# A hybrid decoder layer on one core: the token mix's projections as 2x2 block products in seven multiplications

## The chip, the cores and the metric

The kernel runs on one core of a Trainium2 chip. The metric is the device time of one execution in microseconds (us). Five engines work side by side, each with its own instruction stream: PE (matrix products), DVE and POOL (elementwise work), ACT (copies and activations) and SP, which here only issues DMAs. A core has 16 DMA engines that all queues share.

## The reference, cut to what matters

One layer on 512 prompt tokens and 64 sample tokens (8 sequences of 8), 576 tokens in all, model width 1024, everything in fp32: a half-step SwiGLU feed-forward (FFN1), a token mix, a second feed-forward (FFN2). A conditioning vector gives nine modulation vectors per sequence (`m`, 9 x 1024 columns, 18 strips of 512).

```python
m = silu(c) @ w_ada + b_ada                      # sh1 sc1 g1 sh2 sc2 g2 sh3 sc3 g3
x = x + 0.5 * g1 * swiglu(modulate(rms_norm(x, n1_g), sh1, sc1), w1_gate, w1_up, w1_down)
h = modulate(rms_norm(x, nm_g), sh2, sc2)
z = h @ w_in                                     # 1024 x 10240
u, v, q, k, rv, rg, ga, gb = split(z)            # 1024 1024 1024 1024 2048 2048 1024 1024
o_a = gelu(u) * chunk_spatial_mix(layer_norm(gelu(v)), gm_ws, gm_bs)
o_r, S_new = retention(rotary(q), rotary(k), rv, S0)         # 8 heads, dk 128, dv 256
o_b = head_rms(o_r) * silu(rg)
x = x + g2 * ((sigmoid(ga) * (o_a @ w_a) + sigmoid(gb) * (o_b @ w_b)) @ w_o)
x = x + 0.5 * g3 * swiglu(modulate(rms_norm(x, n2_g), sh3, sc3), w2_gate, w2_up, w2_down)
```

Outputs are the normalised x, the new retention states and the sample rows of the normalised v.

## The kernel before, in words

**Arithmetic.** Activations lie transposed on chip, features on the 128 partitions and tokens along the row. Each fp32 operand is kept as a high and a low part in the PE's faster format (fp32r), and a product is three matmuls: high by high, high by low, low by high. ACT writes the high part (a cast), DVE subtracts to get the low part (L141 and L142 for plain weights, L697 and L707 in the feed-forwards, L149 and L150 for activations). The 576 tokens are taken in two halves of 288, so a block of 128 output columns is 2 x 8 x 3 = 48 matmuls of 128x288 (`proj`, L516, matmul line L522).

**The feed-forwards** already multiply 2x2 blocks. `Operands` builds, once per feed-forward, sums and differences of the four blocks of the activations (1024 features in two halves, 576 tokens in two halves). A `Pair` takes one gate and one up block of 128 columns, forms the sums s1 to s4 of its weight blocks on DVE, and needs seven products P1 to P7 of 12 matmuls (`prod`, L675, matmul line L679) where two `proj` blocks need eight: 84 matmuls for 96. The first two pairs are `Plain`, with eight products, because they come while the operands are still being built. The last product of a pair, p4, is issued only after the next pair's first products.

**The token mix** uses `proj` and two wider forms. Per head (`project`, L1193, eight times): q, k and two blocks of rg by `proj`, 4 x 48 matmuls; then rv with the tokens as the stationary side, 96 matmuls of 128x256 (L1236) and 16 more for the sample tokens (L1244, from the tile `hs`). While head h + 1 is projected, the generator `core` of head h (scores, state update, the norm over the head, the product with silu(rg)) hands out its pieces: each matmul group calls `tick(us)` with a nominal time, and a generator whose pause has run down issues its next piece there. Then `out_b` multiplies head h by its 256 rows of w_b, 16 groups of 6 matmuls, and DVE adds each group to the tile `acc` (L1421, a copy at L1419 for the first head). After the heads, v is made by 192 matmuls of 128x512 and 32 for the sample tokens (L1452), u and the gates ga and gb by `proj` again, and w_a and w_o follow.

**The modulation strips** (`ada_strip`, L295) are a generator too. A strip is four loads of 512 KB, eight groups of matmuls (L265), a copy M by ACT (L271) and four transposes on PE (L277). Two tiles in turn hold loads and copies, so a load waits on its queue until the products of the load two before it are done. Strips 0 to 3 come at the start, 4 and 5 with a pause of 3, strips 6 to 9 in FFN1 with a pause of 12, and 10 to 17 in the token mix with a pause of 20. A strip's generator pauses three and a half times, so at a pause of 12 one lasts about 40 nominal us. `finish(gen)` issues all that is left of a generator at once, with nothing between; `last_down1` (L1098), the last part of FFN1, begins with `finish(rest)`.

**Order.** A scheduler puts each engine's instructions in the order in which the program issues them, apart from three stretches written out by hand as step tables: `BEGIN`, `INTO_MIX` (FFN1's last product, the norm, the operands of the token mix) and `INTO_FFN2`. DMAs issued on SP stand in the program's order and wait there for their buffers. Of a raw weight tile (`wraw`) there are three buffers, of a split one (`whl`) four, and the token mix has one more `whl`.

## Time and profile before

| | |
|---|---|
| time, median of 3 executions | 1718.4 us (1717.9 to 1719.52) |
| the profiled execution | 1718.67 us, its span 1716.6 us |
| PE busy | 1683.7 us (98%), 12588 matmuls |
| DVE busy | 1049.4 us (61%) |
| ACT busy | 686.6 us (40%) |
| POOL busy | 209.0 us (12%) |
| DMA | 199.52 MB, 116 GB/s on average, 38.4% of 16 engines in the main queue |

The span is what the profile records; the execution is 2.1 us longer. FFN1's last products end near 456 us, the heads' projections run from there to about 964 us, then come v, u, the gates and, to about 1255 us, w_a; w_o and FFN2 follow. A matmul's duration overlaps its neighbours', so what a row of matmuls costs is read as the distance from its first start to the next row's start, divided by its count.

### The profile page before, as it was taken

What the parts mean: (1) busy time and instruction counts of PE and PEld (TensorE: products, weight loads), DVE (VectorE), ACT (ScalarE), POOL (GpSimd) and SP (SyncE); (2) the same over time, 40 slices, a digit from 0 to 9 for tenths busy, and PEclk for the clock granted to TensorE, in tenths of its full rate; (3) what the DMA queues carried; (4) which work ended last, traced back from release to release, by engine and by line L of the source; (5) the groups of instructions that cost most, each with busy time, mean ns of one, the idle gap of its engine ahead of it and who ended that gap; (6) DMA issues with size and microseconds to landing.
All of it is one profiled execution on the core that took longest, in us unless ns stands there. A gap on an engine that the chain in (4) does not pass through costs nothing.

```text
span 1716.6 us, 30444 instructions
## 1 busy us (share of the span) xinstructions
PE 1683.7 (98%) x12588; PEld 1610.9 (94%) x12588; DVE 1049.4 (61%) x1758; ACT 686.6 (40%) x1137; POOL 209.0 (12%) x263
## 2 busy tenths in 40 slices
PE   7999999999999999999999999999999999999997
PEld 4879999999999999999999889999999999999997
DVE  6856847676765745745745546422547958666773
ACT  5533524335534333333333333322235525344354
POOL 0000000000421302302202101220021000000002
PEclk9999999999999999999999999999999999999999
DMA  9443444323454433444424335342330323323231
GB/s 301 132 145 98 134 139 129 99 87 95 146 163 140 142 115 125 132 123 125 149 83 143 100 115 161 103 154 75 99 103 21 87 80 92 99 84 89 86 99 56
DMA packets 279773, 199.52 MB, mean 116 GB/s; under 512 B 9801, under 2 KB 253769, under 8 KB 279634
## 3 DMA queue, kind: packets, MB, share of 16 engines
q1 hardware_dynamic: 279634, 197.58, 38.4%
q8 instruction: 98, 1.61, 0.4%
q14 instruction: 41, 0.34, 0.1%
HBM read 183.12 MB, written 14.42 MB: 115 GB/s over the span
## 4 chain that ended last, share of the span: by engine, by line
PE 88%; DVE 4%; DMA 4%; ACT 2%; issue 1%; SPq 0%; POOL 0%; POOLq 0%; DVEq 0%; ACTq 0%
PE ps L522 47%; PE ps L679 24%; PE ps L1236 5%; PE ps L1452 3%; PE ps L265 2%; DMA wraw<-in_w_down_dram 1%; DMA ada<-in_w_ada_dram 1%; DVE whl L707 1%; PE ps L1366 1%; PE ps L1244 1%; PE ps L1328 1%; DMA xa<-in_w_ada_dram 1%; ACT whl L697 1%; PE ps L1372 1%; PE ps L1344 0%
## 5 line engine op out<-in xcount | busy, mean ns | idle before, releaser
L522 PE MATMUL ps<-xa,whl 128*128 128x288 f32 x2784 | 378.4, 295 | 0.5 <-DVE whl L142 0.3
L522 PEld LDWEIGHTS ps<-xa,whl 128*128 128x128 f32 x2784 | 370.9, 188 | 7.6 <-issue 3.4
L679 PE MATMUL ps<-xa,whl 128*128 128x288 f32 x2064 | 292.8, 296 | 1.9 <-ACT whl L697 1.0
L679 PEld LDWEIGHTS ps<-xa,whl 128*128 128x128 f32 x2064 | 279.1, 188 | 10.5 <-issue 2.5
L142 DVE TENSOR_TENSOR whl<-wraw,whl 128x1024 fp32r<-128x1024 f32 x100 | 126.2, 1270 | 212.4 <-ACT whl L141 208.4
L522 PE MATMUL ps<-c,wd 128*128 128x288 f32 x1824 | 246.7, 295 | 0.0
L522 PEld LDWEIGHTS ps<-c,wd 128*128 128x128 f32 x1824 | 243.2, 188 | 2.6 <-issue 1.7
L679 PE MATMUL ps<-xs,whl 128*128 128x288 f32 x1680 | 239.7, 296 | 1.6 <-ACT sn L688 1.4
L679 PEld LDWEIGHTS ps<-xs,whl 128*128 128x128 f32 x1680 | 228.5, 188 | 7.5 <-ACT sn L688 4.9
L522 PE MATMUL ps<-c,whl 128*128 128x288 f32 x1368 | 194.9, 298 | 0.0
L522 PEld LDWEIGHTS ps<-c,whl 128*128 128x128 f32 x1368 | 184.1, 188 | 2.7 <-DVE S L1391 0.8
L141 ACT CAST whl<-wraw 128x1024 fp32r<-128x1024 f32 x100 | 104.0, 1046 | 107.3 <-PE ps L522 47.6
L509 POOL TENSOR_TENSOR x<-x,s 128x64 f32<-128x64 f32 x72 | 34.4, 478 | 909.4 <-DVE s L508 909.2
L503 DVE SCALAR_TENSOR_TENSOR x<-ps,gate,x 128x288 f32<-128x288 f32 (+1 forms) x128 | 61.5, 483 | 135.3 <-PE ps L522 134.9
L697 ACT CAST whl<-sum 128x1024 fp32r<-128x1024 f32 x80 | 84.0, 1050 | 86.3 <-DVE sum L832 58.2
L707 DVE TENSOR_TENSOR whl<-sum,whl 128x1024 fp32r<-128x1024 f32 x80 | 98.0, 1225 | 30.2 <-ACT whl L697 28.2
L697 ACT CAST whl<-wraw 128x1024 fp32r<-128x1024 f32 (+1 forms) x84 | 70.6, 841 | 98.5 <-PE ps L679 84.8
L1236 PEld LDWEIGHTS ps<-whl,xa 128*128 128x128 f32 x768 | 94.1, 194 | 5.1 <-DVE whl L142 3.4
L1236 PE MATMUL ps<-whl,xa 128*128 128x256 f32 x768 | 95.6, 286 | 3.2 <-DVE whl L142 3.2
L909 ACT CAST wd<-wraw 128x640 fp32r<-128x640 f32 (+2 forms) x58 | 45.3, 782 | 123.6 <-PE ps L522 116.7
L707 DVE TENSOR_TENSOR whl<-wraw,whl 128x1024 fp32r<-128x1024 f32 (+1 forms) x84 | 81.2, 967 | 9.5 <-ACT whl L697 9.1
L688 ACT COPY sn<-ps 128x288 f32<-128x288 f32 x126 | 50.1, 398 | 59.2 <-PE ps L679 57.7
(264 smaller groups left out, 1835.2 us busy)
## 6 DMA issues: line engine op xcount, KB each, us to landing
wraw<-in_w_in_dram SPq DMA_DIRECT2D x80, 512.0 KB
ada<-in_w_ada_dram SPq DMA_DIRECT2D x56, 512.0 KB
wraw<-in_w_gate_dram SPq DMA_DIRECT2D x88, 256.0 KB
wraw<-in_w_up_dram SPq DMA_DIRECT2D x88, 256.0 KB
wraw<-in_w_down_dram SPq DMA_DIRECT2D x32, 384.0 KB
wraw<-in_w_down_dram SPq DMA_DIRECT2D x32, 320.0 KB
S<-in_state_ret_dram SPq DMA_DIRECT2D x32, 256.0 KB
wraw<-in_w_b_dram SPq DMA_DIRECT2D x16, 512.0 KB
```

Of the source, the lines that this page charges most:

```text
L141: ACT.copy(out=hi, in_=raw)
L142: (eng or DVE).tensor_tensor(out=lo, in0=raw, in1=hi.bitcast(F32), op=ALU.subtract)
L503: DVE.scalar_tensor_tensor(out=x[:, o:o + w], in0=ps[:, :w], scalar=g[:, c, 0:1], in1=x[:, o:o + w], op0=ALU.mult, op1=ALU.add)
L509: return lambda: POOL.tensor_tensor(out=x[:, NP:T], in0=x[:, NP:T], in1=u, op=ALU.add)
L522: PE.matmul(ps[:, :H], lhsT=s[:, k, c0:c0 + P], rhs=m[:, HALF[h]], start=k == 0 and z == 0, stop=k == kc - 1 and z == 2,)
L679: PE.matmul(ps[:, :H], lhsT=s[:, j * P:(j + 1) * P], rhs=m[:, j, :], start=fresh and j == 0 and z == 0, stop=j == 3 and z == 2, skip_group ...
L688: ACT.copy(out=t, in_=ps[:, :H])
L697: ACT.copy(out=hl[:, 0], in_=src)
L707: DVE.tensor_tensor(out=hl[:, 1], in0=src, in1=hl[:, 0].bitcast(F32), op=ALU.subtract)
L909: ACT.copy(out=hl[:, 0], in_=self.raw[c])
L1236: PE.matmul(ps[:, :DV], lhsT=s, rhs=m, start=i == 0, stop=i == 23)
L1452: PE.matmul(ps, lhsT=s, rhs=m[:, kx % 2, :], start=kx == 0 and z == 0, stop=kx == KC - 1 and z == len(terms) - 1,)
```

## The change

- **Projections.** `Pair2` and `Plain2` extend the feed-forward's classes: the same seven (or eight) products, with the results handed to `out` and `post` in place of gate times up. w_in's 80 column blocks become 40 pairs: q with k, the two rv blocks and the two rg blocks of each head, and neighbouring blocks of u, v, ga and gb. The first two (rg and rv of head 0) are `Plain2`, 38 are `Pair2`. `stream(p)` issues a pair and leaves its last product p4 to be issued by `behind()` inside the next pair, or in `out_b`, `mix` or the w_a products.
- **rv and v** now come out with features on the partitions, like q and k, and PE transposes turn them: 10 per head (`turn_rv`), 40 for v (`turn_v`). ACT copies the results out.
- **Rotary** reads three of a pair's four results from a tile in SBUF that DVE first wrote (`less`), the fourth from PSUM.
- **Operands on chip.** `Operands` for the token mix works in place in x1's tile. x1 is saved to memory before that by 16 DMAs on ACT's queue (steps `sp`), where before 8 DMAs on SP did it later. `Modulate`, `block` and `hs` go. `INTO_MIX` is written anew: it builds the operands and runs the first three pairs.
- **Sums over heads in memory.** `out_b` copies each result with ACT into a tile t (two buffers of 590 KB, 4 groups each) and sends it to the memory tile accd: plain on SP for head 0, with addition on the way on POOL's queue for heads 1 to 7, 28 such DMAs. The 128 DVE operations of L1419 and L1421 go. `gate_b` loads the sums back.
- **Modulation strips.** Strips 6 to 17 all belong to FFN1, with a pause of 8.
- **Weight sums.** S, U and V are written in place into the raw weight tiles, one more DVE operation of 128x512 and one fewer of 128x1024 in every pair, the feed-forwards' too; the tile `sum` goes. The token mix loses its extra `whl`; its raw tiles stay three.

```diff
-    rest = ada_rest(range(6, 10), 12.0)
+    rest = ada_rest(range(6, 18), 8.0)
     start(first_gate, 4.0)
     start(rest, 70.0)
...
         def S(self):
-            self.sum = now["raw"].tile([P, 2, 512], F32, tag="sum", name=nm("sum"), bufs=1)
-            DVE.tensor_tensor(
-                out=self.sum, in0=self.q[:, 1:2].broadcast_to([P, 2, 512]), in1=self.p, op=ALU.add
-            )
+            DVE.tensor_tensor(out=self.p[:, 1], in0=self.q[:, 1], in1=self.p[:, 1], op=ALU.add)
+            DVE.tensor_tensor(out=self.q[:, 1], in0=self.q[:, 1], in1=self.p[:, 0], op=ALU.add)
...
+    class Pair2(Pair):
+        def less(self, i, h, ps, t):
+            out = self.out(i, h)
+            DVE.tensor_tensor(out=out, in0=ps[:, :H], in1=t, op=ALU.subtract)
+            self.post(i, h, out)
...
+    def stream(p, begun=False):
+        if not begun:
+            p.splits()
+            p.p1()
+            p.p1s()
+            p.p2()
+        behind()
+        p.e2()
+        if not begun:
+            p.p5()
+            p.p5s()
+            p.p6()
+            p.p6s()
+        p.p3()
+        p.p7()
+        held.append(p.p4)
...
     def project(hd):
-        ws = w0 if hd == 0 else [load_w(win, 0, KC, head_cols(hd, i), P) for i in range(4)]
+        head = Head(hd) if hd else head0
+        stream(pairs[3] if hd == 0 else head.pair("qk"), hd == 0)
...
-            start(ada_rest(range(10, 18), 20.0), 20.0)
...
+            stream(head.pair("rv"))
+            stream(head.pair("rg"))
+        rv, rvs = turn_rv(head.rv)
...
     def out_b(hd, OB):
         for j in range(2):
             wb = load_w(a["w_b"][0], 2 * hd, 2, j * 512, 512)
             for c in range(4):
+                if c % 2 == 0:
+                    t = tks["tk"].tile([P, 2, T], F32, tag="t", name=nm("t"), bufs=2)
                 for h in range(2):
                     ps = proj(wb, OB, h, kc=2, c0=c * P)
-                    dst = acc[4 * j + c][:, HALF[h]]
+                    behind()
+                    ACT.copy(out=t[:, c % 2, HALF[h]], in_=ps[:, :H])
+                    tick(cost(2))
+                if c % 2:
+                    dst = accd[:, 4 * j + c - 1:4 * j + c + 1, :]
                     if hd == 0:
-                        DVE.tensor_copy(out=dst, in_=ps[:, :H])
+                        nc.sync.dma_start(out=dst, in_=t)
                     else:
-                        DVE.tensor_tensor(out=dst, in0=dst, in1=ps[:, :H], op=ALU.add)
-                    tick(cost(2))
+                        POOL.dma_start(out=dst, in_=t, accum_op=ALU.add)
```

The lines of the changed kernel have other numbers: the strips' products L263, its loads L299, its transposes L275, `prod` L616, `proj` L450, low parts of weights L644, the weight sums S, U and V L754 to L767, `less` L862, rotary L1126 to L1128, the norm over the head L423 to L425 and L1419.

How the strips stand on PE. Before, in FFN1's fourth group, the first half of the last strip (`ada` are its two loads) between the products of the last pairs:

```order
L679 MATMUL ps_3352<-xa_363,whl_3336 128x288 x12
L265 MATMUL ps_3194<-ada_3195,cs 32x512 x2
L265 MATMUL ps_3194<-ada_3196,cs 32x512 x2
L679 MATMUL ps_3375<-xs_78_463,whl_3339 128x288 x12
L679 MATMUL ps_3224<-xa_502,whl_3208 128x288 x12
```

After, on PE at the end of FFN1, the first three rows being the last products ahead of `finish(rest)` (8 of the 12 strips and half of the ninth stand ahead of these rows):

```order
L450 MATMUL ps_4623<-c_4587,wd_4571 128x288
L450 MATMUL ps_4623<-c_4588,wd_4571 128x288
L450 MATMUL ps_4623<-c_4587,wd_4571 128x288
L263 MATMUL ps_4639<-ada_4648,cs 32x512 x2
L263 MATMUL ps_4639<-ada_4649,cs 32x512 x2
L275 MATMUL ps_4658<-ident,ada_4656 128x128 x4
L263 MATMUL ps_4666<-ada_4667,cs 32x512 x2
L263 MATMUL ps_4666<-ada_4668,cs 32x512 x2
L263 MATMUL ps_4666<-ada_4675,cs 32x512 x2
L263 MATMUL ps_4666<-ada_4676,cs 32x512 x2
L275 MATMUL ps_4685<-ident,ada_4683 128x128 x4
L263 MATMUL ps_4693<-ada_4694,cs 32x512 x2
```

The second half of one strip and three whole strips now stand back to back; two more strips of the same form (L263 four times, L275) follow these rows before the next product of FFN1. And on SP, after, the loads for them:

```order
L133 DMA wraw_4761<-in_w_down_dram 128x6x128
L299 DMA ada_4667<-in_w_ada_dram 128x2x512
L299 DMA ada_4668<-in_w_ada_dram 128x2x512
L299 DMA ada_4675<-in_w_ada_dram 128x2x512
L299 DMA ada_4676<-in_w_ada_dram 128x2x512
L299 DMA ada_4694<-in_w_ada_dram 128x2x512
```

Twelve such loads stand together, with no other load among them; the first weights of the token mix come behind the twelfth.

How DVE stands between two heads. Before, where the norm of head 1 (product with silu(rg) L1407, its low parts L150) meets the rotary products of head 2 (L1186 to L1188):

```order
L1407 TENSOR_TENSOR h_6408<-h_6408,h_6397 128x288
L150 TENSOR_TENSOR c_6372<-h_6403,c_6371 128x288
L1186 TENSOR_TENSOR h_6438<-ps_6413,rope 128x288
L150 TENSOR_TENSOR c_6374<-h_6408,c_6373 128x288
L1187 TENSOR_TENSOR h_6439<-ps_6413,rope 64x288
L1188 TENSOR_TENSOR h_6439<-ps_6413,rope 64x288
L282 TENSOR_REDUCE m_6449<-ps_6444 128x36
```

After, the end of the same stretch between heads 5 and 6: it begins with L423 of head 5's norm, 37 rows ahead of the last row here, and holds the sums and low parts for head 6's rv pair (the last of them `whl_9716`) among the rotary of its q and k pair:

```order
L1126 TENSOR_TENSOR h_9695<-h_9692,rope 128x288
L1127 TENSOR_TENSOR h_9696<-h_9692,rope 64x288
L1128 TENSOR_TENSOR h_9696<-h_9692,rope 64x288
L754 TENSOR_TENSOR wraw_9701<-wraw_9702,wraw_9701 128x512
L862 TENSOR_TENSOR c_9769<-ps_9738,sn_9736 128x288
L755 TENSOR_TENSOR wraw_9702<-wraw_9702,wraw_9701 128x512
L1126 TENSOR_TENSOR h_9763<-ps_9594,rope 128x288
L758 TENSOR_TENSOR wraw_9701<-wraw_9701 128x512
L1127 TENSOR_TENSOR h_9764<-ps_9594,rope 64x288
L767 TENSOR_TENSOR wraw_9702<-wraw_9701,wraw_9702 128x512
L1128 TENSOR_TENSOR h_9764<-ps_9594,rope 64x288
L644 TENSOR_TENSOR whl_9716<-wraw_9701,whl_9716 128x1024
```

The four 128x512 sums of the next pair's weights and their low part stand behind the rotary operations; before, DVE had no weight sums in the token mix.

More of the change, by code (lines that the diff above doesn't have):

```diff
@@ L1110, in last_down1 @@
             steps[f"Wl{c}"] = lambda c=c: W.lo(c)
[L1111 to L1120 removed]
+        now["wraw"] = None
+        p = {0: head0.plain("rg", 0), 1: head0.plain("rv", 1), 2: head0.pair("qk")}
+        pairs[3] = p[2]
+        steps.update(operand_steps(O))
+        ends = pair_steps(p, None)
+        for n in ("Gh0", "Gl0", "Gh1", "Gl1", "e1s1", "e1m1"):
+            ends.pop(n)
+        steps.update(ends)
         for c, h in LAST:
@@ L1581, in layer_kernel @@
     second = layer_norm(1, 2.5)
-    for g in range(AHEAD):
-        gate_u(g)
-    gate_b(0)
-    for g in range(8):
-        if g == 1:
-            start(second, 0.0)
+    gate_u(0)
+    gate_u(2)
+    start(second, 0.0)
+    for g in range(0, 8, 2):
         if g == 4:
             finish(second)
+        if g < 4:
+            gate_u(g + 4)
+        else:
+            behind()
         mix(g)
-        if g + AHEAD < 8:
-            gate_u(g + AHEAD)
-        else:
-            gate_b(g + AHEAD - 7)
-    for c in range(4, KC):
-        gate_b(c)
+        mix(g + 1)
+    finish()
     st.close()
```

617 lines of the change are left out of this document (288 added, 329 removed).

## The prediction

> **What bounds the kernel now.** First the page: the span, busy times, slices, the chain.
>
> ```profile
> span 1716.6 us, 30444 instructions
> PE 1683.7 (98%) x12588; PEld 1610.9 (94%) x12588; DVE 1049.4 (61%) x1758; ACT 686.6 (40%) x1137; POOL 209.0 (12%) x263
> PE   7999999999999999999999999999999999999997
> PE 88%; DVE 4%; DMA 4%; ACT 2%; issue 1%; SPq 0%; POOL 0%; POOLq 0%; DVEq 0%; ACTq 0%
> ```
>
> PE is full from the second slice to the last and carries 88% of the chain. A matmul saved is a gain wherever nothing else waits in its place, and any wait put on PE's queue is a loss in full. The profiled execution took 1718.67 us, 2.1 more than its span and 0.3 from the median, so I sum on the span and add 2.1.
>
> Next, the timeline of PE gives the price of each shape: from a row's first start to the next row's start, over its count.
>
> ```profile
> 1204.01 51.04 PE L522 MATMUL ps<-c,whl 128*128 128x288 f32 x384
> 1254.89 12.88 PE L522 MATMUL ps<-xa,whl 128*128 128x288 f32 x96
> ...
> 603.67 11.66 PE L1236 MATMUL ps<-whl,xa 128*128 128x256 f32 x96
> 615.17 2.05 PE L1244 MATMUL ps<-whl,hs 128*128 128x256 f32 x16
> 617.06 1.22 PE L522 MATMUL ps<-c,whl 128*128 128x288 f32 x8
> ...
> 668.81 11.76 PE L1236 MATMUL ps<-whl,xa 128*128 128x256 f32 x96
> ...
> 970.51 11.08 PE L1452 MATMUL ps<-whl,xa 128*128 128x512 f32 x48
> 981.52 1.06 PE L265 MATMUL ps<-ada,cs 128*32 128x512 f32 x8
> ...
> 39.25 0.60 PE L277 MATMUL ps<-ident,ada 128*128 128x128 f32 x4
> 39.60 0.64 PE L679 MATMUL ps<-xa,whl 128*128 128x288 f32 x3
> ```
>
> So 288 wide: 50.88/384 = 0.1325 us. 256 wide: 11.50/96 = 0.120 and 1.89/16 = 0.118. 512 wide: 11.01/48 = 0.229. A transpose: 0.35/4 = 0.09. A head takes 668.81 − 603.67 = 65 us.
>
> **Term 1, the products.** Before, q, k, rg, u, ga and gb are 56 blocks of 48, 2688 matmuls of 288. After, 2 plain pairs of 96 and 38 of 84 make 3384, 696 more: +92.2 us. Gone are 8 x 96 of L1236 (92.0), 8 x 16 of L1244 (15.1) and v's 224 of 512 (51.4): −158.5. Added are 10 transposes a head and 40 for v, 120, at 0.09 to 0.12 (an estimate): +12. Term 1 is **−54 us**; per head, 252 x 0.1325 + 1.0 = 34.4 where 38.8 stood.
>
> **Term 2, the strips at the end of FFN1.** The order shows three and a half strips back to back on PE with nothing between, and twelve loads back to back on SP. Each load waits for one of two tiles, that is for PE or for the copy M. What a load costs when PE waits for it:
>
> ```profile
> 82.10 9.64 SPq L301 DMA_DIRECT2D ada<-in_w_ada_dram  x3
> ...
> 87.62 1.05 PE L265 MATMUL ps<-ada,cs 128*32 128x512 f32 x4 [1.36 <-DMA ada<-in_w_ada_dram]
> 88.60 0.92 PE L679 MATMUL ps<-xs,whl 128*128 128x288 f32 x5
> 90.28 1.05 PE L265 MATMUL ps<-ada,cs 128*32 128x512 f32 x4 [0.76 <-DMA ada<-in_w_ada_dram]
> ...
> 91.38 0.59 ACT L271 COPY ada<-ps 128x512 f32<-128x512 f32 x1 [5.49 <-PE ps L265]
> ```
>
> Issue to use is 5.5 us for the first load of a pair, 8.2 for both, with other loads under way. A strip in the drain is two such round trips, the copy (0.59) and the transposes (0.35): with both at 8.2 it would be 17, with round trips near 4.5, for queues that carry nothing else, 10. I take 12, since the second tile's load overlaps the first tile's products: 3.5 x 12 = 42, less the PE work inside that has to be done anyway (two groups of about 1.0 and 0.35, 2.4 a strip, 8.4). That leaves 34 idle, between 27 and 52. After long gaps the granted clock fell in this trace:
>
> ```profile
> 28.00:32.00 4.00, 2.88 (x10) 1.01 (x12) 3.55 (x8) 4.00 (x7) 0.00 (x0) 0.68 1.00 320
> 32.00:36.00 4.00, 4.00 (x14) 0.78 (x11) 3.49 (x6) 2.94 (x5) 0.00 (x0) 0.89 1.10 304
> ```
>
> That is 4 x 0.32 + 4 x 0.11 = 1.7 us lost. Term 2 is **+35 us** (27 to 53). The eight and a half strips ahead of it, at a pause of 8, come sooner after their loads than at 12: +2 (0 to 6).
>
> **Term 3, DVE between the heads.** Before, DVE has room in a head's 65 us and is nearly idle of weight work; in FFN1, pairs already run on a DVE two thirds busy, without a gap on PE:
>
> ```profile
> 603.00:668.00 65.00, 65.00 (x524) 61.94 (x523) 38.28 (x67) 23.17 (x38) 13.34 (x14) 1.00 0.41 129
> 129.00:172.00 43.00, 43.00 (x326) 43.00 (x325) 28.91 (x47) 15.81 (x24) 2.88 (x6) 1.00 0.35 100
> ```
>
> The rows for what comes and goes:
>
> ```profile
> L707 DVE TENSOR_TENSOR whl<-sum,whl 128x1024 fp32r<-128x1024 f32 x80 | 98.0, 1225 | 30.2 <-ACT whl L697 28.2
> L832 DVE TENSOR_TENSOR sum<-sum,wraw 128x512 f32<-128x512 f32 x40 | 27.6, 690 | 1.0
> ...
> 651.52 0.45 DVE L150 TENSOR_TENSOR c<-h,c 128x288 fp32r<-128x288 f32 x1
> 651.89 0.45 DVE L1407 TENSOR_TENSOR h<-h,h 128x288 f32<-128x288 f32 x1
> ...
> 654.21 0.46 DVE L1187 TENSOR_TENSOR h<-ps,rope 64x288 f32<-64x288 f32 x1
> 654.68 0.45 DVE L1188 TENSOR_TENSOR h<-ps,rope 64x288 f32<-64x288 f32 x1
> 655.16 0.46 DVE L1186 TENSOR_TENSOR h<-ps,rope 128x288 f32<-128x288 f32 x1
> ```
>
> A pair costs DVE three low parts of 1024 (3.7), one of 512 and four sums (3.5) and four results (1.8): 8.9. A head loses eight low parts of 1.22 and 16 additions of 0.45 (L1421, below) and gains three pairs and w_b's two low parts: 38.3 − 9.8 − 7.2 + 26.7 + 2.4 = 50, where PE has 65 − 4.4 and a strip less (2.4), 58. So the mean does not bind; the stretch between two heads does. By starts, a 288 operation takes 0.37, a rotary one 0.47. From the norm's first operation to the low part of the rv pair's sums, DVE has 38: 12 rotary (5.6), 18 of 288 (6.7), three of 128x1024 (about 1.15 when back to back, 3.5), five of 128x512 (about 0.62, 3.1): 18.9 us; at the rows' full durations, 21. PE's norm sums stand six matmuls ahead of the q and k pair, and the products that need that low part begin about 14.2 us after that pair's first. So PE waits 18.9 − 14.2 = 4.7, at full durations 6.8; if half is absorbed by DVE reaching the stretch early, 2.5. The trace has this very case once, at the start of the heads: nine rotary operations in a row ahead of a weight's low part, and PE waits.
>
> ```profile
> 485.58 0.45 DVE L1188 TENSOR_TENSOR h<-ps,rope 64x288 f32<-64x288 f32 x1
> 486.06 4.19 DVE L142 TENSOR_TENSOR whl<-wraw,whl 128x1024 fp32r<-128x1024 f32 x3
> ...
> 487.34 2.93 PE L1236 MATMUL ps<-whl,xa 128*128 128x256 f32 x12 [3.19 <-DVE whl L142]
> ```
>
> Six transitions at 3.7 are 22; heads 0 and 1, which have no earlier head's products to cover them, +4; into v, +1. Term 3 is **+27 us** (10 to 45).
>
> **Term 4, u, the layer norm and the mix.** PE was idle for 1.8 us here, and DVE busy for 34 of 60:
>
> ```profile
> 1040.00:1100.00 60.00, 58.20 (x432) 55.47 (x429) 33.77 (x48) 20.95 (x32) 11.84 (x7) 1.00 0.54 154
> ```
>
> Without about eight plain low parts (9.8) 24 remain, and four u pairs bring 4 x 8.9 = 36: 60, where PE needs four pairs of 84 x 0.1325 and eight mix groups of 1.35 (1059.03 to 1060.38 below), 55. Some of the weights are made ahead of the stretch: **+5** (0 to 12).
>
> ```profile
> 1059.03 1.05 PE L1560 MATMUL ps<-gws,c 128*128 128x128 f32 x8
> 1060.38 6.63 PE L522 MATMUL ps<-xa,whl 128*128 128x288 f32 x48
> ```
>
> **Term 5, sums in memory.** Of the additions that go, all but the first head's took
>
> ```profile
> L1421 DVE TENSOR_TENSOR c<-c,ps x112: 433/448/455, 618.9 to 1032.0; 128x288 f32<-128x288 f32 x112
> ...
> 83.90 0.40 ACT L688 COPY sn<-ps 128x288 f32<-128x288 f32 x1 [0.30 <-PE ps L679]
> ```
>
> 50 us, off the path; ACT gains 128 copies of 0.40, and has 23 of 65 us busy in a head. A tile t is filled by four groups, 24 x 0.1325 = 3.2 us, plus what `core` puts between; the tile two back must have landed within about 4.6 us of its issue on POOL, behind POOL's own operations. No row shows an adding DMA. The nearest is the 512 KB load above at 5.5; PE can run on into free banks for another group or two. So 0 to 1 us for each of 28: **+4**, from 0 to 30. [...]
>
> **The rest.** The way into the token mix: before, PE waited 0.24, 0.56 and the 3.19 above, 4.0 us.
>
> ```profile
> 457.00 4.94 PE L522 MATMUL ps<-xa,whl 128*128 128x288 f32 x35 [0.24 <-DVE xa L463]
> 462.50 0.72 PE L402 MATMUL ps<-all,ones 128*128 128x288 f32 x2 [0.56 <-DVE all L391]
> ```
>
> After, the operands' sums on DVE and ACT stand in the same place, and ACT issues 16 DMAs to save x1; FFN1's last products cover part of it. I take the same 4.0, so nothing, with −4 if all is covered and +5 if ACT's DMAs come late. One small DVE operation more in each feed-forward pair is hidden where 28.9 of 43 us are used; accd's loads ahead of gb have the four ga pairs to arrive in.
>
> **The sum.** 1716.6 − 54 + 35 + 2 + 27 + 5 + 4 = 1735.6, and 2.1: **1738 us**, 1.1% slower.
>
> **Rivals.**
> *DVE keeps up (faster).* What FFN1 shows holds in the heads too: DVE reaches the stretch early and PE's free products cover it. Then term 3 is 5, term 4 is 2, terms 2 and 5 stay near 30 and 1: 1716.6 − 54 + 30 + 2 + 5 + 2 + 1 + 2.1 = 1705. Against it speaks the 3.19 row. It decides where terms 3 to 5 together stay under 17, about 1.5 us a transition.
> *The adding DMAs bind (far slower).* If each takes 2 us longer than its cover, 28 x 2 = 56 replace 4: 1790. For it: only two tiles, and DMAs on POOL stand behind its products. Against it: DMA is 41% busy in a head.
> *No drain.* If loads come faster than I think, or the strips find products to hide behind, 1738 − 35 = 1703. The order speaks against it; it would need the strips apart, so only a small part of the chance goes to it.
>
> **How the numbers follow.** My forecast, 1722 to 1770, gets 0.56; DVE keeping up 0.19 and no drain 0.05, both faster; the DMAs 0.14; the parts cancelling within 0.2%, about what a measurement of this kernel can tell from no change, 0.06. Slower 0.70, same 0.06, faster 0.24. The range leaves one in ten at each end: the bottom just under the second rival's 1705, 1698, and the top short of the DMAs' full price, 1783.
>
> **What would show it.** PE's busy sum falls by about 54. At the end of FFN1 a stretch of some 40 us with PE mostly idle, released by DMA `ada`, four loads to a strip. Between heads, PE gaps of 3 to 5 us released by DVE `whl` or ACT behind it. Under `out_b`, ACT copies into t waiting on POOL's DMAs would show term 5. Gap-free heads, or strips of 6 us, would make me wrong on the fast side; gaps in every `out_b` on the slow side.

## The result and the profile after

The changed kernel takes 1798.36 us (median of 4 runs, 1795.49 to 1805.96) beside 1718.84 us for the kernel before: a ratio of 1.047, 95% interval 1.0436 to 1.0504. It is slower, as forecast, but by 80 us where 20 were forecast, and 15 us above the range. The profiled execution is the fastest of the four.

The page of the changed kernel, the same rows as before:

```profile
span 1793.3 us, 30793 instructions
PE 1680.3 (94%) x12284; PEld 1594.9 (89%) x12284; DVE 1224.9 (68%) x2010; ACT 831.6 (46%) x1455; POOL 249.9 (14%) x301
PE   7999999998699989889889899889999999999997
PEclk9999999999699999999999999999999999999999
PE 80%; DVE 9%; DMA 5%; issue 2%; ACT 2%; POOL 1%; SPq 1%; POOLq 0%; DVEq 0%; ACTq 0%
```

PE has 304 fewer recorded matmuls but nearly the same busy time, so a matmul lasts longer on the average. The slices show two things: one hole (the 6 in the eleventh slice, with the only 6 in PEclk), and after it, through the heads, an 8 in about every second slice. PE's part of the chain falls from 88% to 80%, and DVE's rises from 4% to 9%. What PE waited for, as instruction, what it waited for, us in total, times and the longest:

```profile
PE ps L616 <- DVE whl L644: 27.3, 17, 3.4
PE ps L616 <- ACT whl L634: 24.1, 10, 5.9
PE ps L263 <- DMA ada<-in_w_ada_dram: 22.4, 17, 3.0
```

**Where the 76.7 us of span went.** PE's timeline gives the time at which each stage begins in both kernels (the 425.2 is counted back by matmuls from the row at 427.31 and good to about 0.3 us):

| stage (us) | before | after | change | PE work by term 1 and by strips moved | so lost |
|---|---|---|---|---|---|
| start to the end of FFN1's part ahead of `finish(rest)` | 425.2 | 437.0 | +11.8 | +10.8 (4.5 strips more, 2.4 each) | 1 |
| strips at the end of FFN1 | 0 | 49.6 | +49.6 | +8.4 (3.5 strips) | 41 |
| from there to the first head's products | 31.3 | 36.0 | +4.7 | 0 | 5 |
| heads and v | 575.4 | 594.1 | +18.7 | −35 and −15.6 (6.5 strips less) | 69 |
| u, mix, gates | 172.2 | 164.3 | −7.9 | −19 and −3.6 | 15 |
| w_a to the end | 512.6 | 512.4 | −0.2 | 0 | 0 |

In the heads the −35 are eight times −4.4, +3.2 for head 0's two plain pairs and −2.8 for v. Lost is 131 in all, against −54 from the products. The two largest stages show why. First PE's timeline at the end of FFN1 (start, duration, then in brackets the idle time before the row and what ended it):

```profile
439.96 1.05 PE L263 MATMUL ps<-ada,cs 128*32 128x512 f32 x4 [2.98 <-DMA ada<-in_w_ada_dram]
441.28 1.92 PE L263 MATMUL ps<-ada,cs 128*32 128x512 f32 x4 [0.27 <-DMA ada<-in_w_ada_dram]
443.88 1.11 PE L275 MATMUL ps<-ident,ada 128*128 128x128 f32 x4 [0.69 <-ACT ada L269]
447.14 1.92 PE L263 MATMUL ps<-ada,cs 128*32 128x512 f32 x4 [2.15 <-DMA ada<-in_w_ada_dram]
...
458.38 1.12 PE L275 MATMUL ps<-ident,ada 128*128 128x128 f32 x4 [0.73 <-ACT ada L269]
...
472.18 1.12 PE L275 MATMUL ps<-ident,ada 128*128 128x128 f32 x4 [0.73 <-ACT ada L269]
```

From transposes to transposes a strip takes 14 us. The clock shows in the rows themselves: four products of a strip take 1.05 us in the first row, and 1.92 in nine of the fourteen rows of the stretch. Next the passage between two heads, PE and then DVE:

```profile
713.88 3.46 PE L616 MATMUL ps<-xs,whl 128*128 128x288 f32 x24
717.18 0.69 PE L616 MATMUL ps<-xa,whl 128*128 128x288 f32 x4
720.63 2.55 PE L616 MATMUL ps<-xa,whl 128*128 128x288 f32 x10 [2.77 <-DVE whl L644]
722.98 1.40 PE L616 MATMUL ps<-xs,whl 128*128 128x288 f32 x5
724.18 1.57 PE L616 MATMUL ps<-xa,whl 128*128 128x288 f32 x10
725.59 1.09 PE L616 MATMUL ps<-xs,whl 128*128 128x288 f32 x7
729.01 0.79 PE L616 MATMUL ps<-xa,whl 128*128 128x288 f32 x4 [2.33 <-ACT whl L634]
730.89 4.44 PE L616 MATMUL ps<-xa,whl 128*128 128x288 f32 x20 [1.08 <-DVE whl L644]
735.17 3.35 PE L616 MATMUL ps<-xs,whl 128*128 128x288 f32 x24
...
789.46 2.77 PE L616 MATMUL ps<-xa,whl 128*128 128x288 f32 x10 [2.76 <-DVE whl L644]
```

```profile
708.34 0.46 DVE L423 SCALAR_TENSOR_TENSOR h<-h 128x288 f32<-128x288 f32 x1 [2.33 <-ACT h L421]
...
718.94 1.64 DVE L644 TENSOR_TENSOR whl<-wraw,whl 128x1024 fp32r<-128x1024 f32 x1
...
729.13 0.45 DVE L1128 TENSOR_TENSOR h<-ps,rope 64x288 f32<-64x288 f32 x1
729.61 4.10 DVE L644 TENSOR_TENSOR whl<-wraw,whl 128x1024 fp32r<-128x1024 f32 x3
```

DVE works from 708.34 to past the low part of S with no idle time over 0.4 us, and PE waits three times: 2.77, 2.33 and 1.08, 6.2 us. Ten matmuls behind the first wait take 2.35 us, 0.235 each instead of 0.133, and the twenty behind the third 0.214. A head lasts 789.46 − 720.63 = 68.8 us; its matmuls at full speed take 252 x 0.1325 = 33.4 and its other work about 26 (the heads' 60.75 us in d1 below, with 12 matmuls more and no wait between heads), so about 10 are lost in each: 6.2 of waits, 4 of slow matmuls.

### The profile page after: what moved, and what is told of

It reads as the page before. It is cut to its first block, busy times and chain, and to the rows that moved or that the text cites. A ratio compares the mean times of both kernels' runs of the same rounds, so it can differ in the third digit from the quotient of the medians.

```text
span 1793.3 us, 30793 instructions
## 1 busy us (share of the span) xinstructions
PE 1680.3 (94%) x12284; PEld 1594.9 (89%) x12284; DVE 1224.9 (68%) x2010; ACT 831.6 (46%) x1455; POOL 249.9 (14%) x301
## 4 chain that ended last, share of the span: by engine, by line
PE 80%; DVE 9%; DMA 5%; issue 2%; ACT 2%; POOL 1%; SPq 1%; POOLq 0%; DVEq 0%; ACTq 0%
PE ps L616 45%; PE ps L450 26%; DMA ada<-in_w_ada_dram 2%; PE ps L263 2%; DVE whl L644 2%; DVE h L1419 1%; PE ps L1378 1%; PE ps L1340 1%; DMA xa<-in_w_ada_dram 1%; PE ps L1384 1%; DVE c L153 1%; DMA c<-in_gm_ln_g_dram 1%; PE ps L275 1%; DVE h L1127 0%; DVE h L1128 0%
## 5 line engine op out<-in xcount | busy, mean ns | idle before, releaser
L616 PE MATMUL ps<-xa,whl 128*128 128x288 f32 x4032 | 595.0, 303 | 53.5 <-DVE whl L644 27.3
L616 PEld LDWEIGHTS ps<-xa,whl 128*128 128x128 f32 x4032 | 565.6, 194 | 74.2 <-DVE whl L644 31.6
L616 PE MATMUL ps<-xs,whl 128*128 128x288 f32 x3096 | 446.0, 297 | 7.7 <-DVE c L862 3.1
L644 DVE TENSOR_TENSOR whl<-wraw,whl 128x1024 fp32r<-128x1024 f32 (+1 forms) x318 | 362.9, 1146 | 111.7 <-ACT whl L634 106.3
L616 PEld LDWEIGHTS ps<-xs,whl 128*128 128x128 f32 x3096 | 424.6, 189 | 14.4 <-ACT sn L625 4.5
L634 ACT CAST whl<-wraw 128x1024 fp32r<-128x1024 f32 (+1 forms) x318 | 299.3, 944 | 178.1 <-PE ps L616 108.6
L450 PEld LDWEIGHTS ps<-c,wd 128*128 128x128 f32 x1824 | 243.0, 188 | 4.2 <-ACT wd L917 3.4
L450 PE MATMUL ps<-c,wd 128*128 128x288 f32 x1824 | 246.5, 295 | 0.0
L450 PE MATMUL ps<-c,whl 128*128 128x288 f32 x1368 | 196.6, 298 | 0.0
L450 PEld LDWEIGHTS ps<-c,whl 128*128 128x128 f32 x1368 | 184.6, 188 | 1.7 <-issue 1.4
L1432 ACT COPY t<-ps 128x288 f32<-128x288 f32 x128 | 49.5, 400 | 45.7 <-PE ps L450 34.9
L263 PE MATMUL ps<-ada,cs 128*32 128x512 f32 x224 | 48.3, 690 | 22.4 <-DMA ada<-in_w_ada_dram 22.4
L754 DVE TENSOR_TENSOR wraw<-wraw,wraw 128x512 f32<-128x512 f32 x78 | 55.3, 709 | 6.6 <-DMA wraw<-in_w_in_dram 4.5
L922 DVE TENSOR_TENSOR wd<-wraw,wd 128x640 fp32r<-128x640 f32 (+2 forms) x58 | 53.6, 924 | 8.7 <-ACT wd L917 8.7
L755 DVE TENSOR_TENSOR wraw<-wraw,wraw 128x512 f32<-128x512 f32 x78 | 55.6, 713 | 1.7
L767 DVE TENSOR_TENSOR wraw<-wraw,wraw 128x512 f32<-128x512 f32 x78 | 53.9, 691 | 0.9
```

The lines of the kernel that those rows point to most:

```text
L263: PE.matmul(ps[32 * g:32 * g + 32], lhsT=cs[:, k, :], rhs=w, start=k < 4, stop=k >= 4, tile_position=(0, 32 * g))
L450: PE.matmul(ps[:, :H], lhsT=s[:, k, c0:c0 + P], rhs=m[:, HALF[h]], start=k == 0 and z == 0, stop=k == kc - 1 and z == 2,)
L616: PE.matmul(ps[:, :H], lhsT=s[:, j * P:(j + 1) * P], rhs=m[:, j, :], start=fresh and j == 0 and z == 0, stop=j == 3 and z == 2, skip_group ...
L634: ACT.copy(out=hl[:, 0], in_=src)
L644: DVE.tensor_tensor(out=hl[:, 1], in0=src, in1=hl[:, 0].bitcast(F32), op=ALU.subtract)
L754: DVE.tensor_tensor(out=self.p[:, 1], in0=self.q[:, 1], in1=self.p[:, 1], op=ALU.add)
```

## The experiments

The sum over heads is left out in e3 and d2, the rotary in e7 and d3. All others compute everything. Ratios are to the kernel before on the same chip. Differences in us are to the changed kernel's 1798.36 unless another is named; beside the runs the kernel before took 1718.8 to 1720.7, so they are good to about 2 us.

**Between the heads: what DVE's row is made of.** e7 takes the rotary away, with it POOL's four sums a head, and lets ACT copy the products:

```diff
-        DVE.tensor_tensor(out=t1, in0=src, in1=rope[:, 0, HALF[h]], op=ALU.mult)
...
+        ACT.copy(out=dst[:, HALF[h]], in_=src)
```

> The rotary turn of q and k is left out: ACT copies the products instead, so 12 DVE operations of about 0.47 us a head and POOL's four sums go, and nothing is moved. My theory: DVE's stretch shortens by 6, the waits shrink to under 2 us a head and the clock stays up: a head takes about 61 us, 1798 - 50 = 1748, between 1738 and 1765. Rival A: ACT or the loads hold the weights back, and at most 10 us are gained. Rival B: only the wait shrinks, by 6 x 6 = 36 us, but the clock stays low: 1762 to 1770.

Measured: 1746.86 us, 1.0164 (1.0147 to 1.0181), 51 us less. The waits between heads shrink to these rows:

```profile
710.39 0.80 PE L616 MATMUL ps<-xa,whl 128*128 128x288 f32 x4 [0.31 <-ACT whl L634]
711.65 2.92 PE L616 MATMUL ps<-xa,whl 128*128 128x288 f32 x20 [0.46 <-DVE whl L644]
```

DVE's row from the norm to the low part of S falls from 22.5 to 15.6 us, and a head from 68.8 to 60.5. So most of the 69 us hang on DVE's row between the heads, and the rotary (5.6 us of a row of 22 by its own operations) is enough to undo them. That the place of DVE's operations decides, and not POOL's sums, d1 shows below: it keeps the whole rotary and only moves it on DVE. e5 shortens the row at another place, by giving the rv pair of heads 1 to 7 eight products, which need no sums:

```diff
-            stream(head.pair("rv"))
+            stream8(head.plain("rv", 1))
```

> In heads 1 to 7 the rv pair, whose sums stand in DVE's stretch between two heads, is computed with eight products instead of seven: 12 matmuls more (+1.6 us a head on PE), no S, U, V, two low parts of 1024 instead of three and a half, 5.6 us less on DVE. My theory (DVE's stretch decides): the waits for S's and U's low parts (2.3 and 1.1 us) and part of the slow clock go, the first wait (2.8) stays: about 4 us a head net, 1798 - 27 = 1771, between 1760 and 1785. Rival A (seven products pay as long as PE is the longer engine over a head): slower by 7 x 1.6, 1809. Rival B (clock alone): once a gap remains, the half clock remains too, and only the 3.4 us less 1.6 are gained: 1785 to 1790.

Measured: 1769.41 us, 1.0291 (1.0269 to 1.0313), 29 us less, though PE does 84 matmuls more. One wait is left in a head, 2.31 us for a first half's low part. e6 does the same with all three pairs of heads 1 to 7:

> All three pairs of heads 1 to 7 with eight products: 36 matmuls more a head (+4.8 us on PE), about 17 us less on DVE. Everything else as in the changed kernel. My theory: no wait between the heads is left and the clock stays full, so a head takes 58.5 + 4.8 = 63.3 us instead of 68.8: 1798 - 7 x 5.5 = 1760, between 1750 and 1772, faster although PE does more. Rival A: the seven products are worth what they save, and the time rises by up to 7 x 4.8: 1800 or more. Rival B: the waits come from the weights' loads and stay: 1800 or more too.

Measured: 1774.62 us, 1.0318 (1.0303 to 1.0334): just over its range, 24 us less than the change and no better than e5. The 24 matmuls a head that rg and q and k gain by this, 22 us in seven heads, raise the time by 5: on this DVE seven products bring little there, and lose in rv. e2 changes the order instead, q and k last (and `behind()` ahead of the transposes):

```diff
-        stream(pairs[3] if hd == 0 else head.pair("qk"), hd == 0)
...
+            stream(head.pair("qk"))
```

> The order of the pairs in heads 1 to 7 is rv, rg, qk instead of qk, rv, rg, with the held product of the last pair issued before the scores begin. The same work; the twelve rotary operations leave DVE's stretch between two heads, where PE waited 6.2 us a head and lost another 4 at a lower clock. My theory: DVE's stretch decides, so S's low part comes about 6 us earlier and most of the 10 us a transition goes; the rotary at the end of a head may cost 1 to 4 us there: 1798 - 6 x (10 - 2 - 2) = 1760, between 1750 and 1775. Rival A: DVE is short of time over the whole head, and the wait only moves to the end of the head (scores waiting for rotary): within 8 us of 1798. Rival B: what delays PE is the weights' loads, not the order on DVE: unchanged.

Measured: 1780.99 us, 1.0349 (1.0324 to 1.0374): a miss, 17 us less. A head falls to 65.05 us and the clock stays at 1.00 (each window of 25 us from 625 to 1050 us), but the rotary now stands right ahead of the scores:

```profile
743.24 1.85 PE L616 MATMUL ps<-xs,whl 128*128 128x288 f32 x12 [0.90 <-DVE h L862]
745.35 0.81 PE L1243 MATMUL ps<-ident,h 128*128 128x128 f32 x2 [0.26 <-POOL h L1228]
748.93 1.16 PE L1278 MATMUL ps<-c,c 128*128 128x128 f32 x8 [1.19 <-POOL c L1129]
```

e4 asks how much the slow clock itself costs: products whose results nobody uses (22 and 30 a head) fill PE's gaps.

```diff
+            for i in range(22):
+                PE.matmul(A[:, :H], lhsT=w[:, (i % 4) * P:(i % 4 + 1) * P], rhs=x[:, i % 4, :], start=True, stop=True)
+            rvp.p1(A)
...
```

> In heads 1 to 7, 22 idle products of 128x288 are put ahead of the rv pair's first product and 30 ahead of its fifth, on operands that are there, into banks that the real products overwrite: 52 x 0.1325 = 6.9 us of useless work a head in the place where PE waited 6.2 us and then ran at half clock for about 10 us. My theory: the clock no longer falls, but DVE's last low parts set the end of the stretch, so only the part behind them is gained, 1.7 us of the 3.9 lost to the clock: -10 us, 1788, between 1780 and 1796. Rival A: the clock's loss comes on top of the wait in full, 6 x 3.9: 1775 or less. Rival B: short gaps do not set the clock, and the useless products cost what they do not hide: 1798 to 1815.

Measured: 1790.51 us, 1.0407 (1.0385 to 1.043), 8 us less: as expected. The granted clock is 1.00 in each window of 25 us from 700 to 825 us (0.981 on the mean of the profiled execution, in the changed kernel 0.970), and a head takes 67.25 us instead of 68.8. So of the 4 us of slow matmuls a head, about 1.6 is a loss of its own; it can be a little more, since the idle products run to 731.75 us, 0.6 past the end of S's low part in that run. The rest lies beside DVE's row, for whose end PE has to stand in any case.

**The strips.** e1 lets the strips' generator pause for 5 instead of 8, so that none is left for `finish(rest)`:

```diff
-    rest = ada_rest(range(6, 18), 8.0)
+    rest = ada_rest(range(6, 18), 5.0)
```

> One number is changed: the strips 6 to 17 pause 5 nominal us instead of 8, so that all twelve are done before FFN1's last part and none is left to drain. My theory: the drain's stretch (437.0 to 486.6 us in the trace, 49.6 us, of which about 8 are the strips' own products) disappears, less 0 to 6 us of new short waits for loads inside FFN1: 1798 - 41 = 1757, between 1755 and 1764. Rival A: the loads are bound by the tiles wherever they stand, so the waits only move into FFN1's products: 1785 to 1800. Rival B: the drain also slows what follows it (cold clock, operands late): more than 44 us gained, under 1754.

Measured: 1774.79 us, 1.0305 (1.0277 to 1.0332): 24 us less where 41 were expected, and outside its range: a miss. The stretch is gone; the step into the token mix (L400) comes at 492.87 where it came at 522.21:

```profile
492.87 1.33 PE L400 MATMUL ps<-all,ones 128*128 128x288 f32 x2 [3.90 <-DVE all L389]
PE ps L263 <- DMA ada<-in_w_ada_dram: 5.8, 10, 2.0
```

That is 29 us earlier, of which 24 are left at the end. Of the 49.6 us of the stretch, 20 came back inside FFN1, 8.4 of them the strips' own work. The strips wait for loads there too, in shorter pieces. e8 gives them a third tile:

```diff
-        return adas.tile(list(shape), F32, tag="ada", name=nm("ada"), bufs=2)
+        return adas.tile(list(shape), F32, tag="ada", name=nm("ada"), bufs=3)
```

> Three tiles instead of two for the modulation strips' loads and copies; the drain at the end of FFN1 stays as it is in order. My theory: a strip of the drain took 14 us because each of its five tiles (four loads, one copy) waits for the one two back; with three it takes two thirds, 9.5 us, so 3.5 x 4.7 = 16 us are gained: 1782, between 1775 and 1790. Rival A (the loads are bound by the rate of the DMA engines, or by their own latency in a row): unchanged, 1795 to 1800. Rival B: three tiles also take away most waits inside FFN1: under 1775.

Measured: 1785.63 us, 1.0382 (1.0359 to 1.0404), 13 us less, as expected: a strip of the stretch takes 9.2 to 11.7 us, and the wait for `ada` loads falls from 22.4 to 12.2:

```profile
PE ps L263 <- DMA ada<-in_w_ada_dram: 12.2, 11, 1.8
```

**The sums in memory.** e3 sends every tile t with a plain DMA on SP, so nothing is added:

```diff
-                    else:
-                        POOL.dma_start(out=dst, in_=t, accum_op=ALU.add)
+                    nc.sync.dma_start(out=dst, in_=t)
```

> The tiles t go to memory with a plain DMA on SP for all heads: the addition over heads is left out, and POOL issues no DMA. My theory: the adding DMAs land in 7.1 us in the trace and PE does not wait under the products with w_b, so nothing changes: within 5 us of 1798. Rival (the prediction's, adding DMAs bind): they hold back POOL's rotary sums or ACT's copies, and 10 us or more are gained: under 1788.

Measured: 1787.18 us, 1.038 (1.0358 to 1.0402): a miss, 11 us less. In the changed kernel PE has no wait for t. But an adding DMA keeps POOL for 0.87 us and takes 7.1 to land, and ACT waits 8.1 in all for t (the groups, with mean ns of one and the releasers; then KB and us to landing):

```profile
L1439 POOL DMA_DIRECT2D accd<-t x28 | 24.4, 871 | 142.5 <-ACT t L1432 142.5
L1432 ACT COPY t<-ps 128x288 f32<-128x288 f32 x128 | 49.5, 400 | 45.7 <-PE ps L450 34.9 <-DMA accd<-t 8.1 <-PE ps L1470 2.5
accd<-t POOLq DMA_DIRECT2D x28, 576.0 KB, 7.1
```

Without them PE's waits for DVE's low parts fall from 27.3 to 19.6:

```profile
PE ps L616 <- DVE whl L644: 19.6, 18, 2.0
```

The traces show the way of about half of it. In the changed kernel POOL's issues wait for ACT's copies into t (8.44 us ahead of the one at 704.90, 1.54 ahead of the one at 708.89), POOL's products of the norm (L1418) stand behind them, and one of these then runs beside DVE's L425. In e3 none does:

```profile
709.33 1.62 DVE L425 SCALAR_TENSOR_TENSOR h<-h,h 128x288 f32<-128x288 f32 x1
...
709.50 1.12 POOL L1418 TENSOR_TENSOR h<-c,c 128x288 f32<-128x288 f32 x1
...
710.23 0.46 DVE L425 SCALAR_TENSOR_TENSOR h<-h,h 128x288 f32<-128x288 f32 x1
```

The first two rows are of the changed kernel, the third of e3. The changed kernel has such a long L425 in five of the six passages with a full row on DVE; in e3 L425 takes 0.46 us at most in all its 16 operations, and DVE's row 21.5 us (709.24 to 730.74) instead of 22.5. The rest of the 11 us was not taken apart.

**u.** e9 hands the layer norm of v out between u's pairs instead of all at once ahead of them:

```diff
-    for _ in layer_norm(0):
-        pass
-    second = layer_norm(1, 2.5)
+    first_norm = layer_norm(0, 2.0)
+    second = layer_norm(1, 5.0)
+    start(first_norm, 6.0)
...
+    finish(first_norm)
```

> Only the stage of u is written in another order: the layer norm's two halves are handed out between the products of the u pairs (pauses of 2 and 5 nominal us) instead of the first half ahead of all of them. My theory: there PE waited 3.4 us for a low part and 5.9 us for a high part behind DVE's and POOL's layer norm and mix, some 15 us in all with what follows at a lower clock; half of it goes: 1790, between 1785 and 1796. Rival (DVE and POOL have too much work in this stage, in whatever order): within 4 us of 1798.

Measured: 1797.05 us, 1.0441 (1.0415 to 1.0467): no change that these runs can tell, and the rival's range. In the changed kernel PE waits 3.38 us (up to 1130.62) and 5.91 us (up to 1168.44) here; in e9 the first became two of 2.8 together and the second 2.9. The stage itself, from u's first product to w_a's, took 162.0 us in e9's trace instead of 164.3, but u began 2.5 us later there, ahead of everything that e9 changes. In c1 and d1, which have this order too, the stage takes 159.4.

**Together.** c1 is e5 with three tiles, a pause of 5 and e9's order.

> Together: the rv pair of heads 1 to 7 with eight products, three tiles and a pause of 5 for the strips (no drain), and the new order in the stage of u. If the losses are separate they add up: 1798 - 29 - 33 - 8 = 1728, between 1718 and 1742. Rival: they overlap (what is gained in one place is lost waiting in the next), 1745 or more. Both kernels' mark is 1720.

Measured: 1723.01 us, 1.0016 (1.0006 to 1.0027), within its range: the gains add up. c2 takes e2's order with rg by eight products and the same three.

> As the kernel before it, but heads 1 to 7 in the order rv, rg, qk, and rg (the pair in DVE's stretch) with eight products: neither rotary nor weight sums stand behind the norm. My theory: PE no longer waits between heads, a head takes 60 to 63 us with the scores waiting for rotary at its end, 7 x (68.8 - 62) = 48 instead of 29: 1710, between 1700 and 1728, which would beat the kernel before. Rival: what is gained between heads is lost at their ends, and it comes out as the other combination does, 1725 to 1740.

Measured: 1729.58 us, 1.0054 (1.0039 to 1.0069): a miss; in each head waits of 0.9 and 1.2 us stay at its end, and one of 0.8 to 0.9 behind the norm. c5 is c1 with the first half of rv's weights made ahead of the rotary of q and k (`nh` and `nl` moved into the q and k pair's `stream`).

> As the first combination (rv pair of heads 1 to 7 with eight products, three tiles and a pause of 5 for the strips, the new order in the stage of u), and the first half of the rv pair's weights (high and low part) is made right behind the q and k pair's second product, ahead of the rotary on DVE: an rv pair of two weight tiles needs only one buffer that is free by then. My theory: the wait of 2.3 us that was left between the heads, and the half clock behind it (about 2 us), go: 1723 - 6 x 4 = 1699, between 1692 and 1711, faster than the kernel before by about 1%. Rival A (the clock was not the price, only the wait): 1709. Rival B (DVE is short anyway, the rotary comes late instead): 1720 or more.

Measured: 1720.85 us, 1.0007 (0.9998 to 1.0017): a miss, no faster than before. The wait had only changed its cause, now the subtraction `less` of the q and k pair, seven times 2 us in PE's waits:

```profile
PE ps L616 <- DVE h L862: 13.5, 7, 2.2
```

The last group takes this up. d1 is c5 with the three `less` of a head ahead of its rotary operations:

```diff
+            if self.late is None:
+                self.post(i, h, out)
+            else:
+                self.late.append((i, h, out))
...
         p.p7()
+        for r in p.late or ():
+            p.post(*r)
```

> c5 with one change: the three subtractions (less) of a head's q and k pair all stand ahead of its rotary operations on DVE, where each was followed by its three rotary operations. Theory (c5's 2.25 us a head is p4 of the q and k pair waiting for the third less, which stands behind two rotary groups, 6 x 0.46 = 2.8 us): the 13.5 us of these seven waits go, and with them some of the lost clock: 1706 us (1700 to 1712), faster than the first kernel. Rival (DVE is full from the norm to the rg pair's sums, so what is moved behind the less delays a low part instead): the wait moves to whl L644, 1716 to 1722.

Measured: **1700.12 us, 0.9888 (0.9871 to 0.9906)**, the only kernel here that computes everything and beats the one before. No wait stands between heads, a head lasts 778.22 − 717.47 = 60.75 us, and in the 25 us behind the norm the clock stays at 1.00 though DVE is busy for 21.79 of them:

```profile
717.47 6.55 PE L616 MATMUL ps<-xa,whl 128*128 128x288 f32 x48
724.13 3.46 PE L616 MATMUL ps<-xs,whl 128*128 128x288 f32 x24
727.43 3.36 PE L616 MATMUL ps<-xa,whl 128*128 128x288 f32 x24
730.63 1.76 PE L616 MATMUL ps<-xs,whl 128*128 128x288 f32 x12
...
778.22 6.55 PE L616 MATMUL ps<-xa,whl 128*128 128x288 f32 x48
```

```profile
725.00:750.00 25.00, 24.97 (x188) 24.73 (x187) 21.79 (x38) 11.13 (x18) 9.89 (x10) 1.00 0.46 135
```

d2 and d3 bound c5 from the other side, without the adding DMAs and without the rotary.

> c5 with all sums over heads stored plain on SP's queue, so that the sum over heads is left out (a bound, not a kernel). Theory (POOL's adding DMAs, 0.87 us of issue each, stand ahead of POOL's products in the norm between heads, and so delay DVE's chain there as they did in e3): 6 to 11 us faster than c5, 1710 to 1715. Rival (the chain between heads no longer runs through POOL, since the low parts come ahead of the rotary): 1719 to 1722.

Measured: 1705.52 us, 0.9918 (0.9902 to 0.9933), 15 less than c5 and more than expected; in the changed kernel the same DMAs were worth 11. A head takes 62.1 us instead of c5's 64.7.

> c5 with the rotary left out (ACT copies q and k instead; 12 DVE and 4 POOL operations a head gone): a bound for what DVE's stretch between heads still costs. Theory: the seven waits of 2.25 us and the clock that falls behind them (about 1.3 us a head) go: 1697 us (1690 to 1703). Rival (the heads' loss that is left lies elsewhere, in POOL's and ACT's part of the norm): 1710 or more.

Measured: 1697.51 us, 0.9873 (0.9855 to 0.9891), within its range, and 3 us from d1. Moving the rotary gives nearly all that removing it gives.

d5 moves only the rotary in the changed kernel, seven products and all, behind the rv pair's weight sums.

> The changed kernel with one thing moved and nothing left out: in heads 1 to 7 the rotary operations of three of the four results of the q and k pair stand behind the weight sums and low parts of the rv pair on DVE, and the subtractions (less) ahead of them. Theory (the loss between heads is DVE's row from the norm to the low part of the rv pair's sums): 9 rotary operations of 0.47 = 4.2 us leave that row, so of 6.2 us of waits a head some 2 stay, and most of the clock's 4 us come back: 7 x (4.2 + 2.5) = 47 us less, 1751 us (1742 to 1760). Rival (DVE has too little room over the whole head, so that what is put off makes the rg pair's low parts or the scores late): 1775 to 1795.

Measured: 1780.08 us, 1.0355 (1.0336 to 1.0373): a miss; the rival's range, though not at the place that the rival named, for at the rg pair PE waits 0.61 us only. The first wait of a passage is gone, but the four sums and their low part still end after the products that cover them:

```profile
724.24 0.80 PE L616 MATMUL ps<-xa,whl 128*128 128x288 f32 x4 [1.03 <-ACT whl L634]
726.49 4.46 PE L616 MATMUL ps<-xa,whl 128*128 128x288 f32 x20 [1.45 <-DVE whl L644]
```

d6 adds to d5 the three tiles and the pause of 5 for the strips, and e9's order.

> The same with three strip tiles, a pause of 5 for the strips and the layer norm between u's pairs, as in c1: what the full change of seven products gives when the three terms are mended by order alone. Theory: c1 stood 46 us under e5 by these, so 1751 - 46 = 1705 us (1697 to 1712); if no wait were left between heads it would be 12 x 0.1325 x 7 = 11 us under d1, 1689. Rival as for the run before: 1730 to 1750.

Measured: 1731.57 us, 1.0078 (1.0066 to 1.0091), the rival's range again. d1 beats it by 31 us with 84 matmuls more on PE: in both places where it was tried (the change beside e5, and d6 beside d1, which also makes rv's first weights ahead of the rotary) rv is better off with eight products.

## Why the prediction was wrong, and where it was right

The sign and the main mechanisms were right; the size was wrong, 131 us lost where 73 were added. Of the 58 between them, 38 are in the heads.

- **Term 1 (−54): right.** Where nothing waits, a pair takes what the sum says. A pair of the gates, from its first row to the next pair's first row, takes 11.2 us:

```profile
1224.92 3.36 PE L616 MATMUL ps<-xa,whl 128*128 128x288 f32 x24
...
1236.12 3.36 PE L616 MATMUL ps<-xa,whl 128*128 128x288 f32 x24
```

  84 x 0.1325 is 11.1. The sign "PE's busy sum falls by about 54" was no good: it fell by 3.4, with the granted clock at 0.97 on the mean instead of 0.996, for slow matmuls fill it up again. Counting matmuls and reading a gap-free pair would have been better signs.
- **Term 2 (+35, 27 to 53): right in kind, 6 short.** 41 measured; a strip takes 14 us and not 12. Round trips were even as short as the lower bound had them, with its 4.5 us that no row quoted there shows: in the last strip of the stretch (472 to 486 us) the second and the fourth load take 4.6 and 3.6 us from issue to first product. But the working had left out the strip's own products, which stand between them and took 1.9 us twice at the slow clock, and the transposes take 1.1 and not 0.35: 4.6 + 1.9 + 3.6 + 1.9 + 0.7 + 1.1 = 14. The clock was priced at 1.7 us by the one early stretch quoted, and it stood near 0.6 on the mean of the stretch:

```profile
437.00:486.60 49.60, 27.64 (x73) 5.12 (x73) 4.21 (x12) 5.36 (x10) 1.83 (x2) 0.62 0.59 172
```

  The 2 us for the strips ahead were about 1. e1 shows what the term did not ask: spread out, the same strips still cost 12 us more than their work.
- **Term 3 (+27, 10 to 45): the step that failed, by its size.** The place, the row on DVE and the releaser were as forecast; e7, e5 and d1 show it. The working took 3.7 us a passage, near the mean of 4.7 (18.9 − 14.2) and of the 2.5 for the case that half is absorbed. Nothing was absorbed, and the row was longer: from the norm's first operation to the end of the low part of S, DVE took 708.34 to about 730.85, 22.5 us. By the term's own subtraction 22.5 − 14.2 = 8.3 are lost in a passage.
  - The 38 operations that had been counted are all there. Of the 3.6 us above 18.9, 2.7 are five operations that ran beside one of POOL's, and 0.8 is idle time. Over the whole trace, 179 low parts of 128x1024 with no operation of POOL beside them took 1.23 us at most; 61 with one took up to 2.19, 1.45 on the mean. That POOL is the cause is shown for L425 alone, by e3; for the others it is this coincidence.
  - To this come slow matmuls behind the row: the twenty behind the third wait take 4.28 us, where 20 x 0.1325 = 2.65, 1.6 more. The prediction counted the clock for strips alone.
  - The six passages with a full row are 68.7 us apart on the mean. d1's are 60.75, 59.2 without its 12 matmuls more, so 9.6 are lost in each and 57 in all, of the 69 in the heads, where terms 3 and 5 had 31. About 9 of the others d1 loses too (below).
- **Term 4 (+5, 0 to 12): too small,** 15 measured. Two waits came, 3.38 us for a low part on DVE and 5.91 for a high part on ACT. e9 made them shorter, and the stage by 2.3 us in its trace.
- **Term 5 (+4, 0 to 30): the size fits, the way doesn't.** It looked for ACT copies and PE waiting for t. Of e3's 11 us about half come through DVE's row instead, by L425 beside POOL. A transfer takes 7.1 us from issue to landing (median; 5.8 to 9.5), more than the 4.6 that the term allowed it; ACT waits for t six times, 8.1 us in all, and PE never.
- **The way into the token mix (0, −4 to +5): at its upper end,** 4.7. The wait is 3.91 us for the norm's sums on DVE in place of 0.56.
- **The rivals.** "DVE keeps up" and "no drain" did not happen. "The adding DMAs bind" gave 1790, near the result by chance: its mechanism is worth 11.

Still open: d1 stands about 25 us above its own sum without waits (1716.6 − 54 + 11 = 1674, its span 1698.4). Of these, 5 lie ahead of the heads (its first product there comes at 480.50, before at 456.46, 19.2 of the difference being strips); 9 lie in the heads and v (544.7 us, where the sum has 536) and 10 in u, mix and gates (159.4 for 149.6). They were not taken apart.

## What to carry to other kernels

Seven products for eight trade matmuls on PE for a row of sums on DVE, and the mean load of DVE (68%) says nothing about it: ask at each place what DVE has to do between the weights' arrival and the first product that needs the sums, at full durations, and try eight products where that row is longer than the products that cover it. A postprocessing step that nobody waits for, as the rotary here, belongs behind the low parts and subtractions that PE waits for; moving it gave within 3 us what deleting it gave. Work that waits for its own loads (the strips) belongs where there are products to run meanwhile: spread out, the last strips cost 12 us beyond their own work and not 41, and a third tile for the loads was worth 13 us. And look at what POOL does beside such a row: DVE's L425 took 1.62 us beside a product of POOL's and 0.46 without.

## What the chip showed that was not expected

Behind some of the short waits between heads the matmuls ran slower. Of the 23 windows of 25 us from 550 to 1125 us, nine hold waits between heads or lie right behind them and have a granted clock of 0.86 to 0.95; the other fourteen have 1.00 (the changed kernel; stretch, its length, busy time and count of PE, PEld, DVE, ACT and POOL, then the clock, the DMA share and GB/s):

```profile
650.00:675.00 25.00, 19.85 (x122) 19.30 (x123) 21.93 (x31) 8.23 (x11) 8.32 (x10) 0.86 0.18 51
725.00:750.00 25.00, 21.59 (x150) 21.12 (x149) 19.27 (x25) 11.91 (x18) 6.15 (x7) 0.93 0.34 103
750.00:775.00 25.00, 25.00 (x213) 23.78 (x212) 14.17 (x24) 14.74 (x35) 5.40 (x6) 1.00 0.57 130
```

From 721 to 724 us the granted clock is 0.50, and ten matmuls stand 0.235 us apart instead of 0.133. The length of the wait does not decide alone: such slow matmuls followed a wait of 2.77 us and one of 1.99, and behind one of 3.11 us (599.71 to 602.82) the clock stayed at 1.00. What else decides, no run here shows. Of the time that this takes, e4 gave back 8 us.
